# Expert weights in rows of 8 KB, gate products ahead of up products, and two sets of transposes moved

## The chip, the cores and the metric

The kernel runs on one core of a Trainium2 chip. The metric is the device time of one execution in microseconds (us). Three runs of the kernel before gave 740.38, 738.9 and 739.66 us.

## The reference

One decoder block and a final norm, for 256 tokens of width 1024, in float32. The first half is adaptive RMSNorm, one input projection (5120 columns), two kinds of attention with 8 heads each, gated branches and an output projection. The second half, cut to what matters here:

```python
h2 = modulate(rms_norm(x, g2), shift2, scale2)
scores = sigmoid(h2 @ w_router)              # 64 experts in 8 groups, the best 4 groups, the best 8 experts
for each expert e, for the tokens that chose it:
    y[e] = (silu(h2 @ w_gate[e]) * (h2 @ w_up[e])) @ w_down[e]   # 1024 -> 256 -> 1024
moe = sum over e of weight[token, e] * y[e] + the same with one shared expert
out = rms_norm(x + gate2 * moe, final_g)
```

The weights of one expert are three matrices of 1 MB each, so the 64 experts read 192 MB.

## The kernel before

**Tiles.** The chosen (token, expert) pairs are put into slots. 26 tiles hold 128 slots each: most take two experts with 64 slots each, every fourth or fifth takes four experts with 32 slots (tile 3, 7, 11, 15, 20 and 25), some take one of 96 and one of 32. Which expert has how many slots is decided on the chip by rank. `groups(i)` lists the column ranges of a tile: two groups of 64, or four of 32.

**A tile's work**, in the loop at the end of the file: `tile_up` (L1131, TensorE) multiplies the tile's gathered tokens `hl` with the gate and up weights into one PSUM buffer `gu` of 512 columns, 256 for each; `swiglu` (ACT L1003, DVE L1004) makes the gated values `sg`; `slot_map` (L1141 and DVE) makes the tile's scatter matrix; `scatter` (L1187) adds the results of the tile before to the sums; `gather(i + 1)` (L1071, 96 short bf16 matmuls) collects the tokens of the next tile, copied out by `hl<-rot` on ACT and DVE (L1075, L1077); `hidden_T` (L1016) transposes `sg`, and DVE copies it to `at` (L1019); `down` (L1155) multiplies `at` with the down weights. In tile 0 the gather of tile 1 stands behind `down`. `extra` adds the ranking in tile 0, the shared expert's transposes in tile 1, its end in tile 11, and the ranking of late experts in tile 15. The shared expert's up products (`shared_up`, L1011) run earlier, with the attention's last work.

**Weights.** `w8()` hands out buffers of 1 MB (8 KB on each of 128 partitions) in a ring, first 9 and in the expert part 20 of them; some are buffers of earlier work (`vv`, `hh`, `g2r`, `gr`, `sr`, `xs`, `whi`, `wlo`), which come free when that work is done. All weight DMAs are issued by SyncE (SP) in the order of the program. At most 8 of them are in flight, since each waits for the one eight ahead of it. SP waits before a DMA until the ring's buffer is free, and everything behind it waits too.

**The start.** `mod_sums(j)` (L360) adds the conditioning vector's products, each with 1 MB of weights; `shift_scale` copies the sums on ACT (L366) and turns them with short matmuls (L370); `turned(j)` (L351) transposes two blocks of the first tokens; `modulated(j)` applies shift and scale (ACT L381, DVE); `row_hi` and `row_lo` split the projection weights into two parts (L392 and DVE), and `proj_row` (L272, L273, L275) multiplies. Their order is a written list, `do(...)`.

Of the kernel before, what the change touches and what calls it, by code (L numbers as in the profile page):

```python
# [9 lines left out]
F32 = mybir.dt.float32  # L10
# [4 lines left out]
AF = mybir.ActivationFunctionType  # L15
# [10 lines left out]
FF = 256  # L26
# [82 lines left out]
def block_kernel(ctx: ExitStack, tc: tile.TileContext, x, c, norm1_g, norm2_g, w_ada, b_ada, w_in,  # L109
                 w_branch_sb, w_branch_mb, w_out, w_router, router_bias, w_gate_e, w_up_e, w_down_e,  # L110
                 w_gate_sh, w_up_sh, w_down_sh, rel_bias, final_g, const_a, const_m, const_b, out):
    nc = tc.nc
    P = 128
    mm = nc.tensor.matmul
# [4 lines left out]
    wk = ctx.enter_context(tc.tile_pool(name="wk", bufs=1))  # L119
# [7 lines left out]
    def w8():  # L127
        ring.append(ring.pop(0))
        return k8(ring[-1], [P, 2048])
# [27 lines left out]

    ss2 = consts.tile([P, 10], F32, name="ss2")

    def load_gu(wg, wu, h):  # L160
        w = w8().rearrange("p (g j f) -> p g j f", g=2, j=4)
        nc.sync.dma_start(w[:, 0], wg.rearrange("(p j) f -> p j f", j=8)[:, 4 * h:4 * h + 4])
        nc.sync.dma_start(w[:, 1], wu.rearrange("(p j) f -> p j f", j=8)[:, 4 * h:4 * h + 4])
        return [w[:, :, j, :] for j in range(4)]

    def load_dn(wd):
        w = w8().rearrange("p (j n) -> p j n", j=2)
# [3 lines left out]
    h2, h2v, hp3, r1, h2T, scores_ = [], [], [], [], [], []  # L171
# [31 lines left out]
    with ExitStack() as pa:  # L203
        ps = pa.enter_context(tc.tile_pool(name="ps", bufs=2, reuse_waits="tile", space=PSUM))

        def big():
            return ps.tile([P, 512], F32, name="big", tag="big", bufs=4)
# [92 lines left out]
        graw, rows = {}, {}  # L300
# [53 lines left out]
        def mod_sums(j):  # L354
# [4 lines left out]
            for n in range(4):  # L359
                mm(rows["m"][32 * n:32 * n + 32, :], cpad[:, j, :], w[:, 512 * n:512 * n + 512], start=j == 0,  # L360
                   stop=j == 7, skip_group_check=True)

        def shift_scale():

            sb = wk.tile([P, 512], F32, name="adasb", tag="ada", bufs=2)
            nc.scalar.activation(sb, rows.pop("m"), AF.Copy)  # L366
            p = big()
            firsts = ident.rearrange("p (n r) -> p n r", r=32)[:, :, 0]
            for k in range(4):
                mm(p[:, 4 * k:4 * k + 4], sb[:, 128 * k:128 * k + 128], firsts, start=True, stop=True,  # L370
                   skip_group_check=True)
            p = p[:, 0:16].rearrange("p (k i u) -> p i u k", k=4, i=2)
            m = modq.rearrange("p (u k) i -> p u k i", u=2)
            bq = biasq.rearrange("p (u k) i -> p u k i", u=2)
            nc.vector.tensor_tensor(m[:, :, :, 1], p[:, 0], bq[:, :, :, 1], op=OP.add)
            nc.vector.tensor_tensor(m[:, :, :, 0], p[:, 1], bq[:, :, :, 0], op=OP.add)
            nc.vector.tensor_tensor(modq[:, :, 2], modq[:, :, 0], gb[:, 0:8], op=OP.mult)
# [312 lines left out]
        def do(f, *args, keys=()):  # L690
            plan.append((keys, lambda: f(*args)))
# [5 lines left out]
        do(mod_sums, 2, keys=[("adk", 2)])  # L697
        do(columns, keys=[("ca",)])
        for j in range(3, 8):
            if j > 3:  # L700
                do(turned, 2 * j - 8)
            do(mod_sums, j, keys=[("adk", j)])
        do(shift_scale)
        do(modulated, 0)
        do(row_hi, 0, keys=[("inj", 0)])
        do(row_lo, 0)
# [32 lines left out]
        for i, ticks in enumerate(ROW_AT):  # L739
            n = 4 + i  # L740
# [214 lines left out]
    def late_expert(k):  # L955

        no = sm("no", [1, 2], I32)
        nc.sync.dma_start(no[:, 0:1], ranks_d[:, bass.ds(k, 1)])
        rank_ = nc.values_load(no[0:1, 0:1], engines=[EN.SP], min_val=0, max_val=NE - 1)
        nc.sync.dma_start(no[:, 1:2], order_d[:, bass.ds(rank_, 1)])  # L960
        col = sm("col", [P, 4])
        nc.sync.dma_start(col, late_d[:, bass.ds(rank_, 1)].rearrange("p o q -> p (o q)"))
        ev = nc.values_load(no[0:1, 1:2], engines=[EN.SP], min_val=0, max_val=NE - 1)
        wg, wu, wd = (w[0, bass.ds(ev, 1)].rearrange("o a b -> (o a) b") for w in (w_gate_e, w_up_e, w_down_e))
        gu = load_gu(wg, wu, 0) + load_gu(wg, wu, 1)
        wd = load_dn(wd)
        for first in (0, 128):
            one = small().rearrange("p (t s) -> p t s", t=4)[:, 0:2]
            for t in range(NT):
                nc.vector.tensor_scalar(one[:, t], iota1, float(first), col[:, t:t + 1], op0=OP.add, op1=OP.is_equal)  # L970
            S = wk.tile([P, NT, 128], BF, name="S", tag="zs", bufs=4)
            nc.vector.tensor_copy(S, one)
            xg = gather(len(TILES), S)
            pq = rot()
            for t in range(NT):
                nc.tensor.transpose(pq[:, t * 128:(t + 1) * 128], one[:, t], ident)
            for t in range(NT):
                mm(pq[:, 256:257], one[:, t], col[:, 2 + t:3 + t], start=t == 0, stop=t == 1, skip_group_check=True)
            ST = wk.tile([P, 256], F32R, name="ST", tag="e", bufs=3)
            wsl = sm("wsl", [P, 1], bufs=2)  # L980
            nc.vector.tensor_copy(ST, pq[:, 0:256])
            nc.vector.tensor_copy(wsl, pq[:, 256:257])
            p = gub()
            for j in range(8):
                mm(p, xg[:, j], gu[j], start=j == 0, stop=j == 7)
            at = hidden_T(swiglu(p))
            scatter(ST, down(at, [wd], [(0, 128, 0)], wsl))

    shp, shw = {}, {}

    def load_shared():
        shw["gu"] = load_gu(w_gate_sh[0], w_up_sh[0], 0) + load_gu(w_gate_sh[0], w_up_sh[0], 1)

    def load_shared_down():
        shw["d"] = load_dn(w_down_sh[0])
# [11 lines left out]
    def shared_up(t, j0, j1):  # L1007
        if j0 == 0:
            shp[t] = rot() if t else gub()
        for j in range(j0, j1):  # L1010
            mm(shp[t], h2T[0][:, j, t * 128:(t + 1) * 128], shw["gu"][j], start=j == 0, stop=j == 7)  # L1011

    def hidden_T(sg, at=None):
        pt = rot()
# [73 lines left out]
    def load_tile(i):  # L1088
        n = len(TILES[i])
        es = []  # L1090
        for _, r in TILES[i]:
            if r < NFIX:
                es.append([w[0, r] for w in (w_gate_e, w_up_e, w_down_e)])
            else:
                ev = nc.values_load(order[0:1, r:r + 1], engines=[EN.SP], min_val=0, max_val=NE - 1)
                es.append([w[0, bass.ds(ev, 1)].rearrange("o a b -> (o a) b") for w in (w_gate_e, w_up_e, w_down_e)])
        if i == len(TILES) - 1:

            gu = [load_gu(e[0], e[1], 0) for e in es]
            ws = [w8().rearrange("p (g j f) -> p g j f", g=2, j=4) for e in es]  # L1100
            for j in (0, 2):
                for w, e in zip(ws, es):
                    for g in range(2):
                        nc.sync.dma_start(w[:, g, j:j + 2],
                                          e[g].rearrange("(p j) f -> p j f", j=8)[:, 4 + j:6 + j])
            for g, w in zip(gu, ws):
                g += [w[:, :, j, :] for j in range(4)]
            return gu, load_dn_cuts([e[2] for e in es])
        gu = [[] for s in range(n)]
        for h in range(2):  # L1110
            for s in range(n):
                gu[s] += load_gu(es[s][0], es[s][1], h)
        return gu, [load_dn(e[2]) for e in es]

    def groups(i):

        out, c0 = [], 0
        for s, (cap, _) in enumerate(TILES[i]):
            for n in (32, 32, 32) if cap == 96 else (cap,):
                out.append((c0, n, s))  # L1120
                c0 += n
        return out

    def tile_up(i, xg, gu, between=()):
        p = gub()
        for j in range(8):
            if j == 4:
                for f in between:
                    f()
            for c0, n, s in groups(i):  # L1130
                mm(p[c0:c0 + n, :], xg[:, j, c0:c0 + n], gu[s][j], start=j == 0, stop=j == 7, skip_group_check=True)  # L1131
        return swiglu(p)

    def slot_map(i):
# [87 lines left out]
    S = slots(0)  # L1222
# [11 lines left out]
    xg = gather(0, S)  # L1234
# [40 lines left out]
    for i in range(len(TILES)):  # L1275
        if i == SH_AT:
            load_shared_down()
        gu, wd = load_tile(i)
        last = i == len(TILES) - 1
        if last:  # L1280
            fin, res = final_row()
            ST, wsl = slot_map(i)
            sg = tile_up(i, xg, gu, [lambda: scatter(*prev), lambda: final_gain(fin)])
            nc.scalar.preload_act_table_set("sqrt_and_others")
        else:
            sg = tile_up(i, xg, gu, () if i else [by_expert])
            S = slots(i + 1)
            ST, wsl = slot_map(i)
            if prev:
                scatter(*prev)  # L1290
            if i:
                xg = gather(i + 1, S)
        at = hidden_T(sg)
        for f in extra.get(i, ()):
            f()
        if last:
            last_down(at, wd, groups(i), wsl, ST)
        else:
            prev = ST, down(at, wd, groups(i), wsl)
            if i == 0:  # L1300
                xg = gather(i + 1, S)
    final_norm(fin, res)
    pc.close()

# [30 lines left out]
```

## Time and profile before

| | |
|---|---|
| median of 3 runs | 739.66 us |
| lowest, highest | 738.9, 740.38 us |
| the profiled execution | 740.37 us |
| its span in the trace | 738.6 us |
| TensorE busy | 691.3 us (94%) |
| TensorE's mean granted clock | 0.989 |
| bytes by DMA | 266.73 MB, mean 361 GB/s |

The span is the time from the first to the last instruction that the profiler saw; the execution is 1.8 us longer. A resource that is busy 94% of a span need not be the one that ends last in each stretch of it, so the rows below go by stretches.

### The profile page before, as it was taken

The page shows a single profiled execution, that of the slowest core. Times are in us where ns is not written, and L with a number is a line of the kernel's source. Part 1 is how long each engine was busy: PE and PEld are TensorE (multiplying, and loading weights), DVE is VectorE, ACT ScalarE, POOL GpSimd, SP SyncE. Part 2 cuts the span into 40 slices and gives each one's busy share as a digit, 9 for nine tenths or more (in the row PEclk, how much of TensorE's full clock was granted, in tenths as well). Part 3 has the DMA queues.
Part 4 walks back from the last instruction along what each step waited for, and adds up shares of the span by engine and source line. Part 5 has one row for each costly group of instructions (what it writes and reads, how often), then busy time and mean ns, then how long its engine had stood idle before and what let it go on. Part 6 is the DMA issues. An engine that isn't in the chain of part 4 may idle for free.

```text
span 738.6 us, 12518 instructions
## 1 busy us (share of the span) xinstructions
PE 691.3 (94%) x4743; PEld 384.3 (52%) x4743; DVE 316.2 (43%) x667; ACT 202.2 (27%) x332; POOL 16.0 (2%) x33
## 2 busy tenths in 40 slices
PE   3899999999999999999999999999989998899994
PEld 0486677676888546444444454344444553355532
DVE  1366766666576833333333333233233332233323
ACT  2344666555835521111111111111111111111122
POOL 1010001000001000000000000000000000000000
PEclk9899999999999999999999999999999999999998
DMA  9999988777567699999999999999999999999994
GB/s 354 412 385 387 364 271 301 251 269 273 177 235 269 259 375 416 354 389 412 409 415 414 413 390 412 411 412 412 416 413 412 412 412 415 412 411 408 402 335 158
DMA packets 76862, 266.73 MB, mean 361 GB/s; under 512 B 7013, under 2 KB 9221, under 8 KB 67968
## 3 DMA queue, kind: packets, MB, share of 16 engines
q1 hardware_dynamic: 75344, 262.24, 91.7%
q0 software_dynamic: 1312, 3.65, 1.5%
q8 instruction: 39, 0.64, 0.4%
q14 instruction: 23, 0.19, 0.1%
q10 hardware_dynamic: 144, 0.00, 0.0%
HBM read 264.68 MB, written 1.19 MB: 360 GB/s over the span
## 4 chain that ended last, share of the span: by engine, by line
PE 51%; DMA 45%; DVE 2%; ACT 1%; issue 0%; SPq 0%; DVEq 0%; ACTq 0%
DMA w<-in_w_up_e_dram 17%; PE gu L1131 9%; PE big L272 7%; PE big L275 7%; PE big L273 7%; DMA wlo<-in_w_up_e_dram 7%; DMA sr<-in_w_down_e_dram 5%; PE rot L1155 4%; DMA w<-in_w_down_e_dram 4%; DMA hh<-in_w_down_e_dram 4%; DMA w<-in_w_ada_dram 4%; PE rot L1071 3%; DMA gr<-in_w_up_e_dram 3%; PE acc L1187 3%; PE att L420 2%; DMA hh<-in_w_gate_e_dram 2%
## 5 line engine op out<-in xcount | busy, mean ns | idle before, releaser
L1131 PE MATMUL gu<-w,hl 128*32 128x512 f32 (+1 forms) x568 | 99.0, 594 | 2.4 <-DMA w<-in_w_up_e_dram 2.0
L272 PE MATMUL big<-whi,hh 128*128 128x512 f32 x184 | 75.2, 409 | 1.7 <-ACT whi L392 1.7
L273 PE MATMUL big<-whi,hl 128*128 128x512 f32 x184 | 72.9, 396 | 0.0
L1004 DVE TENSOR_TENSOR sg<-sg,gu 128x256 f32<-128x256 f32 x27 | 11.4, 421 | 138.7 <-ACT sg L1003 138.7
L1071 PE MATMUL rot<-S,qksb 128*128 128x128 bf16 x624 | 69.1, 219 | 0.0
L1071 PE MATMUL rot<-S,qkmb 128*128 128x128 bf16 x624 | 68.7, 219 | 0.0
L1167 ACT ACTIVATE mg<-y 128x512 fp32r<-128x512 f32 x51 | 32.1, 629 | 130.2 <-DVE y L1161 130.2
L1161 DVE SCALAR_TENSOR_TENSOR y<-rot,wsl,gate 128x512 f32<-128x512 f32 (+1 forms) x53 | 39.1, 738 | 65.0 <-PE rot L1155 63.1
L1131 PEld LDWEIGHTS gu<-w,hl 128*32 128x32 f32 (+1 forms) x568 | 29.9, 121 | 60.9 <-issue 58.8
L1155 PE MATMUL rot<-w,at 128*32 128x512 f32 (+1 forms) x256 | 56.2, 610 | 5.7 <-DVE at L1019 5.7
L254 DVE TENSOR_TENSOR wlo<-w,whi 128x2048 fp32r<-128x2048 f32 x23 | 52.7, 2291 | 20.1 <-ACT whi L253 19.1
L275 PE MATMUL big<-wlo,hh 128*128 128x512 f32 x184 | 54.2, 395 | 0.2 <-DVE wlo L254 0.2
L1187 PE MATMUL acc<-mg,ST 128*128 128x512 f32 x204 | 54.0, 406 | 0.0
L1168 DVE TENSOR_TENSOR mg<-y,mg 128x512 fp32r<-128x512 f32 x51 | 35.3, 692 | 38.4 <-ACT mg L1167 38.4
L1075 ACT ACTIVATE hl<-rot 128x512 f32<-128x512 f32 x26 | 15.5, 597 | 120.8 <-PE rot L1071 120.8
L1003 ACT ACTIVATE sg<-gu 128x256 f32<-128x256 f32 x27 | 10.4, 383 | 138.5 <-PE gu L1131 138.5
L1071 PEld LDWEIGHTS <-qksb 128*128 128x128 bf16 x624 | 42.6, 98 | 7.8 <-issue 6.7
L1187 PEld LDWEIGHTS acc<-mg,ST 128*128 128x128 f32 x204 | 36.3, 188 | 17.4 <-ACT sg L1003 9.1
L253 ACT ACTIVATE whi<-w 128x2048 fp32r<-128x2048 f32 x23 | 43.9, 1909 | 5.0 <-PE big L273 5.0
L272 PEld LDWEIGHTS big<-whi,hh 128*128 128x128 f32 x184 | 35.1, 191 | 17.1 <-issue 3.8
L1071 PEld LDWEIGHTS <-qkmb 128*128 128x128 bf16 x624 | 43.6, 98 | 0.0
L275 PEld LDWEIGHTS big<-wlo,hh 128*128 128x128 f32 x184 | 34.8, 190 | 8.4 <-DVE wlo L254 0.6
(352 smaller groups left out, 1055.7 us busy)
## 6 DMA issues: line engine op xcount, KB each, us to landing
w<-in_w_gate_e_dram SPq DMA_DIRECT2D x60, 512.0 KB, 12.1
w<-in_w_up_e_dram SPq DMA_DIRECT2D x60, 512.0 KB, 12.6
w<-in_w_down_e_dram SPq DMA_DIRECT2D x26, 1024.0 KB, 12.5
w<-in_w_ada_dram SPq DMA_DIRECT2D x24, 1024.0 KB, 11.6
w<-in_w_in_dram SPq DMA_DIRECT2D x16, 1024.0 KB, 12.4
whi<-in_w_gate_e_dram SPq DMA_DIRECT2D x12, 512.0 KB, 11.3
whi<-in_w_up_e_dram SPq DMA_DIRECT2D x12, 512.0 KB, 11.7
wlo<-in_w_down_e_dram SPq DMA_DIRECT2D x6, 1024.0 KB, 11.3
```

The source lines that it names most:

```text
L253: nc.scalar.activation(hi, w, AF.Copy)
L254: nc.vector.tensor_tensor(lo, w, hi.bitcast(F32), op=OP.subtract)
L272: mm(p, aa[i][0], ww[i][0], start=start and i == 0, stop=False)
L273: mm(p, aa[i][1], ww[i][0], start=False, stop=False)
L275: mm(p, aa[i][0], ww[i][1], start=False, stop=stop and i == n - 1)
L1071: mm(p[:, b * 128:(b + 1) * 128], hp3[k // 3][k % 3][:, half * 4 + b, :], S[:, k // 3], start=k == 0, stop=k == 5)
L1131: mm(p[c0:c0 + n, :], xg[:, j, c0:c0 + n], gu[s][j], start=j == 0, stop=j == 7, skip_group_check=True)
L1155: mm(py[c0:c0 + w, 0:n], at[:, jj, c0:c0 + w], wd[s][:, jj, o:o + n], start=jj == 0, stop=jj == 1, skip_group_check=True)
L1161: nc.vector.scalar_tensor_tensor(y, py[:, 0:n], wsl, gate2[:, o:o + n], op0=OP.mult, op1=OP.mult)
L1167: nc.scalar.activation(yh, y, AF.Copy)
L1168: nc.vector.tensor_tensor(yl, y, yh.bitcast(F32), op=OP.subtract)
L1187: mm(sums(t, c), m if len(y) > 1 else m.bitcast(F32), part, start=False, stop=stop and k == len(y) - 1, skip_group_check=True)
```

## The change

1. `load_gu` gives the gate and the up matrix of an expert a 1 MB buffer each, and moves each with one DMA whose rows are 8 KB long. Before, a buffer held half of both: two DMAs of 512 KB with rows of 4 KB. `load_tile` issues all gates of a tile, then all ups, then the downs. For the last tile the ups come in pieces of 4, 2 and 2 of the 8 blocks.
2. `up_cut` makes the products with 256 columns each, all eight gate blocks first, then the eight up blocks; before, each product had 512 columns (gate and up side by side).
3. In the start, the first `turned` goes ahead of `mod_sums(4)`, the other three behind the last `mod_sums`, around `shift_scale`, whose copy on ACT is a step of its own (`mod_copy`).
4. `hidden_T` stands ahead of `gather(i + 1)`, in all tiles, and tile 0's gather for tile 1 ahead of its ranking and its `down`.

```diff
-    def load_gu(wg, wu, h):
-        w = w8().rearrange("p (g j f) -> p g j f", g=2, j=4)
-        nc.sync.dma_start(w[:, 0], wg.rearrange("(p j) f -> p j f", j=8)[:, 4 * h:4 * h + 4])
-        nc.sync.dma_start(w[:, 1], wu.rearrange("(p j) f -> p j f", j=8)[:, 4 * h:4 * h + 4])
-        return [w[:, :, j, :] for j in range(4)]
+    def load_gu(wg, wu):
+
+        ws = [w8().rearrange("p (j f) -> p j f", j=8) for _ in range(2)]
+        for w, d in zip(ws, (wg, wu)):
+            nc.sync.dma_start(w, d.rearrange("(p j) f -> p j f", j=8))
+        return ws
+
+    def up_cut(p, xg, gu, gs, k):
+
+        g, j = divmod(k, 8)
+        for c0, n, s in gs:
+            mm(p[c0:c0 + n, FF * g:FF * g + FF], xg[:, j, c0:c0 + n], gu[s][g][:, j, :], start=j == 0, stop=j == 7,
+               skip_group_check=True)
...
         for j in range(3, 8):
-            if j > 3:
-                do(turned, 2 * j - 8)
+            if j == 4:
+                do(turned, 0)
             do(mod_sums, j, keys=[("adk", j)])
+
+        do(mod_copy)
+        do(turned, 2)
         do(shift_scale)
+        do(turned, 4)
+        do(turned, 6)
         do(modulated, 0)
...
-            gu = [load_gu(e[0], e[1], 0) for e in es]
-            ws = [w8().rearrange("p (g j f) -> p g j f", g=2, j=4) for e in es]
-            for j in (0, 2):
-                for w, e in zip(ws, es):
-                    for g in range(2):
-                        nc.sync.dma_start(w[:, g, j:j + 2],
-                                          e[g].rearrange("(p j) f -> p j f", j=8)[:, 4 + j:6 + j])
-            for g, w in zip(gu, ws):
-                g += [w[:, :, j, :] for j in range(4)]
+            gu = [[w8().rearrange("p (j f) -> p j f", j=8) for g in range(2)] for e in es]
+            for g, o, m in ((0, 0, 8), (1, 0, 4), (1, 4, 2), (1, 6, 2)):
+                for w, e in zip(gu, es):
+                    nc.sync.dma_start(w[g][:, o:o + m], e[g].rearrange("(p j) f -> p j f", j=8)[:, o:o + m])
             return gu, load_dn_cuts([e[2] for e in es])
-        gu = [[] for s in range(n)]
-        for h in range(2):
-            for s in range(n):
-                gu[s] += load_gu(es[s][0], es[s][1], h)
+        gu = [[w8().rearrange("p (j f) -> p j f", j=8) for g in range(2)] for e in es]
+        for g in range(2):
+            for w, e in zip(gu, es):
+                nc.sync.dma_start(w[g], e[g].rearrange("(p j) f -> p j f", j=8))
...
-            if i:
-                xg = gather(i + 1, S)
         at = hidden_T(sg)
+        if not last:
+            xg = gather(i + 1, S)
         for f in extra.get(i, ()):
             f()
         if last:
             last_down(at, wd, groups(i), wsl, ST)
         else:
             prev = ST, down(at, wd, groups(i), wsl)
-            if i == 0:
-                xg = gather(i + 1, S)
```

`shared_up`, the late expert's products and `tile_up` call `up_cut` in a loop over k from 0 to 15.

SP's DMAs for tile 2 and the first of tile 3, before (tile 2's two experts lie in `hh`, `g2r` and two buffers of `gr`; tile 3 begins at `vv`):

```order
L162 DMA hh<-in_w_gate_e_dram 128x1024
L163 DMA hh<-in_w_up_e_dram 128x1024
L162 DMA g2r<-in_w_gate_e_dram 128x1024
L163 DMA g2r<-in_w_up_e_dram 128x1024
L162 DMA gr_2449<-in_w_gate_e_dram 128x1024
L163 DMA gr_2449<-in_w_up_e_dram 128x1024
L162 DMA gr_2452<-in_w_gate_e_dram 128x1024
L163 DMA gr_2452<-in_w_up_e_dram 128x1024
L168 DMA sr<-in_w_down_e_dram 128x2048
L168 DMA xs<-in_w_down_e_dram 128x2048
```

The same place now:

```order
L1122 DMA hh<-in_w_gate_e_dram 128x2048
L1122 DMA gr_2483<-in_w_gate_e_dram 128x2048
L1122 DMA g2r<-in_w_up_e_dram 128x2048
L1122 DMA gr_2484<-in_w_up_e_dram 128x2048
L176 DMA sr<-in_w_down_e_dram 128x2048
L176 DMA xs<-in_w_down_e_dram 128x2048
L1122 DMA vv<-in_w_gate_e_dram 128x2048
L1122 DMA w_2671<-in_w_gate_e_dram 128x2048
L1122 DMA w_2673<-in_w_gate_e_dram 128x2048
L1122 DMA w_2675<-in_w_gate_e_dram 128x2048
L1122 DMA w_2670<-in_w_up_e_dram 128x2048
L1122 DMA w_2672<-in_w_up_e_dram 128x2048
```

The DMA into `g2r` now stands behind the first one into `gr`, and a tile's buffers are no longer filled in the order of the ring: `w_2675`, the seventh buffer from `vv` on, is filled fourth.

TensorE at the start, before (`big` takes the sums of `mod_sums`, `att<-ca` are the transposes of `turned`, `big<-ca` those of `shift_scale`):

```order
L360 MATMUL big<-w_112,cpad 32x512 x4
L351 MATMUL att<-ca,gr_102 128x128 x4
L360 MATMUL big<-w_114,cpad 32x512 x4
L351 MATMUL att<-ca,gr_102 128x128 x4
L360 MATMUL big<-w_116,cpad 32x512 x4
L351 MATMUL att<-ca,gr_102 128x128 x4
L360 MATMUL big<-w_118,cpad 32x512 x4
L351 MATMUL att<-ca,gr_102 128x128 x4
L360 MATMUL big<-w_125,cpad 32x512 x4
L370 MATMUL big<-ca,adasb 128x4 x4
```

The same place now:

```order
L368 MATMUL big<-w_112,cpad 32x512 x4
L359 MATMUL att<-ca,gr_102 128x128 x4
L368 MATMUL big<-w_114,cpad 32x512 x4
L368 MATMUL big<-w_116,cpad 32x512 x4
L368 MATMUL big<-w_118,cpad 32x512 x4
L368 MATMUL big<-w_125,cpad 32x512 x4
L359 MATMUL att<-ca,gr_102 128x128 x4
L380 MATMUL big<-ca,adasb 128x4 x4
L359 MATMUL att<-ca,gr_102 128x128 x8
L280 MATMUL big<-whi,hh 128x512
```

Twelve of the sixteen transposes now stand behind the last of the sums, four of them ahead of the short matmuls and eight behind.

TensorE in an early tile, before: the end of the gather (`qkmb` and `qksb` are halves of the tokens' values), the transposes of `sg`, and the first of the down products (`gr` holds down weights here):

```order
L1071 LDWEIGHTS qkmb_1943
L1071 MATMUL rot<-S,qkmb_1943 128x128
L1016 MATMUL rot<-ca,sg 128x128 x2
L1155 MATMUL rot<-gr_2833,at 32x512 x3
L1155 MATMUL rot<-gr_2835,at 32x512
```

The same tile now, from the end of the scatter on:

```order
L1196 MATMUL acc_1948<-mg,ST 128x512
L1196 MATMUL acc_1950<-mg,ST 128x512
L1031 MATMUL rot<-ca,sg 128x128 x2
L1086 LDWEIGHTS qksb_1804
L1086 MATMUL rot<-S,qksb_1804 128x128
```

The two transposes moved from behind the gather to ahead of it.

## Rows read from the trace of the kernel before

**Rows 1.** The page: DMA's busy tenths in 40 slices of the span.
```profile
DMA  9999988777567699999999999999999999999994
```

**Rows 2.** Windows: us, busy of PE, PEld, DVE, ACT, POOL; PE clock; DMA share; GB/s.
```profile
264.00:324.00 60.00, 57.60 (x414) 27.59 (x409) 19.69 (x48) 7.86 (x15) 0.00 (x0) 0.97 1.00 384
324.00:684.00 360.00, 342.16 (x2760) 164.78 (x2759) 116.84 (x263) 44.80 (x80) 1.09 (x2) 1.00 1.02 411
...
700.00:712.00 12.00, 11.48 (x91) 5.11 (x89) 4.53 (x9) 1.86 (x3) 0.20 (x1) 1.00 0.92 318
```

**Rows 3.** The chain that ended last, one tile: start us, us, what.
```profile
655.40 6.87 PE gu L1131 x32
...
664.97 2.70 PE rot L1071 x48
668.47 3.65 PE rot L1155 x16
672.13 6.87 PE gu L1131 x32
```

**Rows 4.** Waits of TensorE: us in total, times, longest us.
```profile
PE rot L1155 <- DVE at L1019: 10.9, 21, 0.5
...
PE gu L1131 <- DMA w<-in_w_up_e_dram: 2.0, 2, 1.5
```

**Rows 5.** Timeline of TensorE: first up products of tiles 0, 1, 11, 12, 25.
```profile
261.21 1.08 PE L1131 MATMUL gu<-w,hl 128*64 128x512 f32 x4
...
280.42 2.01 PE L1131 MATMUL gu<-w,hl 128*64 128x512 f32 x8 [0.39 <-DVE hl L1077]
...
448.83 1.49 PE L1131 MATMUL gu<-w,hl 128*32 128x512 f32 x12
...
474.63 0.64 PE L1131 MATMUL gu<-wlo,hl 128*64 128x512 f32 x1
...
706.15 1.06 PE L1131 MATMUL gu<-w,hl 128*32 128x512 f32 x8
```

**Rows 6.** Windows: no weights in flight; 4 KB rows alone; a slow patch; 8 KB alone.
```profile
252.00:256.50 4.50, 4.50 (x18) 2.14 (x17) 3.98 (x9) 0.74 (x1) 0.00 (x0) 1.00 0.02 4
...
381.00:389.00 8.00, 8.00 (x84) 2.32 (x76) 2.04 (x3) 1.39 (x3) 0.00 (x0) 1.00 1.03 410
441.00:445.00 4.00, 3.73 (x54) 3.23 (x52) 1.12 (x4) 0.53 (x1) 0.00 (x0) 1.00 1.00 296
453.00:457.00 4.00, 4.00 (x42) 1.30 (x34) 0.16 (x1) 0.39 (x1) 0.00 (x0) 1.00 1.01 422
```

**Rows 7.** Timeline of SP: DMA issues into three buffers.
```profile
243.94 0.33 SPq L162 DMA_DIRECT2D g2r<-in_w_gate_e_dram  x1
...
255.87 0.33 SPq L162 DMA_DIRECT2D gr<-in_w_gate_e_dram  x1
...
279.50 0.33 SPq L162 DMA_DIRECT2D w<-in_w_gate_e_dram  x1
```

**Rows 8.** Timeline of TensorE: passes of 256 columns in the last tile's down.
```profile
723.78 0.40 PE L1155 MATMUL rot<-hh,at 128*32 128x256 f32 x1
...
724.02 0.38 PE L1155 MATMUL rot<-hh,at 128*32 128x256 f32 x1
...
724.24 0.59 PE L1155 MATMUL rot<-hh,at 128*32 128x256 f32 x2
```

**Rows 9.** Timeline of TensorE: attention's last matmuls, first and seventh of a run.
```profile
236.93 0.39 PE L273 MATMUL big<-late,hl 128*128 128x512 f32 x1
...
238.31 0.39 PE L273 MATMUL big<-late,hl 128*128 128x512 f32 x1
```

**Rows 10.** Timeline of TensorE, and a window: the start.
```profile
29.01 1.45 PE L370 MATMUL big<-ca,adasb 128*128 128x4 f32 x8 [0.72 <-ACT adasb L366]
...
32.11 0.79 PE L272 MATMUL big<-whi,hh 128*128 128x512 f32 x1 [1.65 <-ACT whi L392]
...
31.00:34.30 3.30, 2.19 (x5) 1.45 (x6) 2.65 (x6) 3.30 (x7) 0.00 (x0) 0.50 1.03 411
```

More of the change, by code (lines that the diff above doesn't have):

```diff
@@ L361, in mod_sums, with mod_copy @@
                    stop=j == 7, skip_group_check=True)
+        def mod_copy():
+            sb = rows["c"] = wk.tile([P, 512], F32, name="adasb", tag="ada", bufs=2)
+            nc.scalar.activation(sb, rows.pop("m"), AF.Copy)
         def shift_scale():
-            sb = wk.tile([P, 512], F32, name="adasb", tag="ada", bufs=2)
-            nc.scalar.activation(sb, rows.pop("m"), AF.Copy)
-            p = big()
+            sb, p = rows.pop("c"), big()
             firsts = ident.rearrange("p (n r) -> p n r", r=32)[:, :, 0]
@@ L964, in late_expert @@
         wg, wu, wd = (w[0, bass.ds(ev, 1)].rearrange("o a b -> (o a) b") for w in (w_gate_e, w_up_e, w_down_e))
-        gu = load_gu(wg, wu, 0) + load_gu(wg, wu, 1)
+        gu = load_gu(wg, wu)
         wd = load_dn(wd)
@@ L983, in late_expert @@
             p = gub()
-            for j in range(8):
-                mm(p, xg[:, j], gu[j], start=j == 0, stop=j == 7)
+            for k in range(16):
+                up_cut(p, xg, [gu], [(0, 128, 0)], k)
             at = hidden_T(swiglu(p))
@@ L991, in load_shared @@
     def load_shared():
-        shw["gu"] = load_gu(w_gate_sh[0], w_up_sh[0], 0) + load_gu(w_gate_sh[0], w_up_sh[0], 1)
+        shw["gu"] = load_gu(w_gate_sh[0], w_up_sh[0])
     def load_shared_down():
@@ L1009, in shared_up @@
             shp[t] = rot() if t else gub()
-        for j in range(j0, j1):
-            mm(shp[t], h2T[0][:, j, t * 128:(t + 1) * 128], shw["gu"][j], start=j == 0, stop=j == 7)
+        for k in range(2 * j0, 2 * j1):
+            up_cut(shp[t], h2T[0][:, :, t * 128:(t + 1) * 128], [shw["gu"]], [(0, 128, 0)], k)
     def hidden_T(sg, at=None):
@@ L1125, in tile_up @@
         p = gub()
-        for j in range(8):
-            if j == 4:
+        for k in range(16):
+            if k == 8:
                 for f in between:
                     f()
-            for c0, n, s in groups(i):
-                mm(p[c0:c0 + n, :], xg[:, j, c0:c0 + n], gu[s][j], start=j == 0, stop=j == 7, skip_group_check=True)
+            up_cut(p, xg, gu, groups(i), k)
         return swiglu(p)
```

## Prediction

> **What bounds the kernel now.** I read the page first: TensorE is busy for 94% of the span (the table), and the DMA row shows nines until slice 7, a thinner middle, and nines again from slice 14 to 38 [rows 1]. So two resources are nearly full, and which of them ends last has to be read by stretch. Then the stretches of the expert part: DMA share 1.00 from 264 to 324, 1.02 from 324 to 684 at 411 GB/s, and 0.92 at 318 GB/s when the last tile's pieces are issued [rows 2]. A share of 1.00 says that the sixteen engines always have packets; only a faster packet or a smaller total can shorten that stretch.
>
> TensorE is as near. A tile with no wait takes 672.13 - 655.40 = 16.73 us [rows 3]: products up 6.87, the scatter of the tile before 2.0, the next tile's gather 2.70, a gap, the down products 3.65. The gap is the step on which the third part of the change works: the gather ends at 664.97 + 2.70 = 667.67 and the down products start at 668.47; between them lie two transposes and the wait for DVE's copy of them, 21 times and 10.9 us in all [rows 4]. From tile 0 (261.21) to tile 25 (706.15) pass 444.94 us [rows 5]; 25 tiles of 16.73 would be 418.25. Of the 26.7 over, tile 0 has 280.42 - 261.21 - 16.73 = 2.5, and tile 11 with the shared expert's end 474.63 - 448.83 - 16.73 = 9.1. Of the 15.1 left I put 3 on other inserted work (an estimate: the shared transposes and the late-expert ranking) and **12 on waiting for weights**. The waits view's largest row of such waits has only 2.0 us [rows 4], because a matmul that starts late between its neighbours counts as busy; I trust the starts.
>
> So TensorE waits for weights late, while the DMA queue never rests: **the end is set by the weight stream**, with TensorE about 12 us behind it as the second bound.
>
> **The change, part by part.** The base is the profiled execution, 740.37 us (0.7 over the median of the runs, 739.66; I subtract it at the end).
>
> *Weights in 8 KB rows.* The trace has stretches with one kind alone: 410 GB/s where all in flight are gate and up halves with 4 KB rows, 422 where all are down weights with 8 KB rows [rows 6]. For 1 MB (1,048,576 bytes) that is 2.557 us against 2.485, 0.073 us less. The stream's steady part moves two of these for each expert of tiles 3 to 24 (54 experts), two for tile 2, four for the last tile: about 114 MB. 114 x 0.073 = **-8.3 us**. The bounds are 0 (row length is not the cause, only which weights they are) and -8.3.
>
> *Slow patches.* In 441 to 445 the 4 KB rows ran at 296 GB/s [rows 6], 4 x (1 - 296/410) = 1.1 us lost; the pure down stretch shows none. From 324 to 684 a third of the bytes at 422 and two thirds at 410 would be 414; at 411 some 360 x 3/414 = 2.6 us are lost. In 264 to 324, 384 against 414 is 4.3 more, part of which is plain shortage of free buffers. I take half of the 2.6: **-1.3**, with bounds 0 and -6.9.
>
> *Order of issue.* Now all gates go out before the first up. In tile 2 the second expert's gate goes into `gr`, and the first expert's up into `g2r` behind it on SP. Before, `g2r` was filled from 243.94 and `gr` from 255.87, when the product that reads `gr` was done [rows 7]; between them the DMA engines have nothing (0.02 in 252 to 256.5, [rows 6]). The 1 MB of `g2r` used to pass before this hole; now it waits behind `gr`, and comes after it: one MB at 2.5 us, **+2.5** (0 if a buffer further on would have stopped the stream for as long anyway). In tile 3 the fourth gate takes the buffer of tile 0's first down weights; the DMA for that buffer left at 279.50 before [rows 7], and will be the fourth of the tile instead of the sixth pair, with seven others of its tile behind it. Tile 0's down will be earlier by the 2 us of its own gap, so I count **0**, between -2 and +2.
>
> *Last tile.* Its gates go as 1 MB, the ups in 4 x 512 KB and 8 x 256 KB, where 16 pieces of 256 KB were. The stretch 700 to 712 lost 12 x (1 - 318/410) = 2.7 us [rows 2]; half the small pieces are gone, but the end is still cut fine: **-1**, between 0 and -2.7.
>
> *Halved matmuls.* Each up product now runs as 16 steps of 256 columns instead of 8 of 512, per expert group. A 512-column pass (an f32 product is two records) takes 6.87/16 = 0.43 us. The trace has 256-column passes with the same 32-column f32 weights in the last tile's down: 723.78, 724.02, 724.24 [rows 8], so 0.24 for the first and 0.22 for the next, against 0.215 for half of 0.43. I take 3 ns on 32 passes, 0.1 us per tile; the upper bound is 0.24 in all, 0.85 per tile. A rule speaks against this part: the Trainium skill, "TensorEngine Tiling (Array Packing)", section "Instruction Overhead", gives each matmul some 60 cycles of overhead, which is 25 ns at 2.4 GHz, and by it the 32 added passes of a tile would cost 0.8 us, 21 us in all; the second pass of the row above shows at most 5 ns. In `shared_up`, with 128-column weights, the weight load is longer: the nearest rows, one load of 128 columns for each matmul, start (238.31 - 236.93)/6 = 0.23 apart [rows 9], where a 256-column pass that hides its load takes 0.215. 64 passes x 0.015 = **+1.0** (0 to 1.0), and it is on the path, since `gr` is freed by these products.
>
> *Transposes ahead of the gather.* TensorE's wait for `at` (10.9 us) goes under the gather, and tile 0 loses up to its 2.5. On TensorE alone -13.4; but this engine waits for weights anyway, so its gain becomes a longer wait for weights: **0** in the sum. It frees each buffer a little earlier, which the full queue can't use. If the queue had room, this would be the gain.
>
> *First tokens' transposes.* TensorE stands idle for 0.72 and 1.65 us while ACT copies the sums and makes the first weights' parts [rows 10]; four transposes go into the first gap and eight into the second. Before, twelve of the sixteen ran between sums that wait for the weights' DMA, where they cost nothing, so only an earlier rise of the granted clock (0.50 in 31 to 34.3, where the first projection matmuls start [rows 10]) can gain: **-0.5**, between -2 and +1 (if `modulated` has to wait for the last of them).
>
> Sum: -8.3 - 1.3 + 2.5 + 0 - 1 + 1.0 + 0 - 0.5 = **-7.6**: 740.37 - 7.6 = 732.8, and less the 0.7, **732**.
>
> Does TensorE stay under it? It could end 10.9 + 2.5 + 12 - 1.0 - 26 x 0.1 = 22 us earlier if no weight wait were left. I leave it 3 us of them (the four-expert tiles want 12 MB at once). 19 against 7.6: yes.
>
> **Rivals.** *A, TensorE becomes the bound (the other side).* If a 256-column pass with two 64-column groups, which no row of before shows in f32 with 128 rows, costs x more per tile, TensorE's work ends the kernel at 740.37 - (10.9 + 2.5 + 12 - 1.0) + 3 + 26x. That passes 732.8 at x = 0.53 and the time before at x = 0.82, near the first pass of [rows 8] at all 32 (0.85). At x = 1.0 it gives 745.0, less 0.7, 744. For it: the 0.24; against it: the 0.22 after it. Chance 0.08. (By the Trainium skill's 0.8 us a tile, above, this sum would give 739.)
>
> *B, the rate does not rise.* The 422 may belong to something else in those stretches than the length of a row, and the order of issue still holds the queue up: 740.37 + 2.5 - 1 + 1.0 - 0.5 - 0.7 = 741.7. With the hold-up hidden too, 739. For it: short stretches say little on cause; against it: gate, up and down weights lie in the same memory and go to the same buffers, and differ in the row. Chance 0.12.
>
> *C, slow patches belong to 4 KB rows and all go.* -6.9 in place of -1.3: 732 - 5.6 = 726.4. For it: no 8 KB stretch has one; against: the pure 8 KB stretches are short. Chance 0.15.
>
> **How the numbers follow.** The forecast has 0.65, A 0.08, B 0.12, C 0.15. A measurement of this kernel tells about 0.2% (1.5 us) from no change. The forecast's own range, from its bounds, is 728 to 737; with C at one end and half of B at the other it is 726.5 to 739.5. Faster: all of the forecast and C and a little of A: 0.82. Same: half of B and a third of A, 0.09. Slower: 0.09.
>
> **What would show it.** The windows of 324 to 684 near 420 GB/s with the share still at 1.0; the wait of the down products for DVE's copy gone, and more waits of up products for up weights instead; the tile period still 16.8 where nothing is waited for (17.6 would be A); SP's `g2r` issue after `gr`, about 256. A rate of 411 would make me wrong by B, and rows of up products waiting for nothing but running to the end by A.

## The result, and the profile after

| | before | after |
|---|---|---|
| median, us | 739.28 (4 runs, 738.42 to 740.38) | 728.72 (4 runs, 726.94 to 729.78) |
| the profiled execution, us | 740.37 | 728.46 |
| its span, us | 738.6 | 726.7 |

The ratio is 0.9854, with a 95% interval of 0.983 to 0.9878: 10.6 us faster, 1.5%. The forecast was 732 and 7.6 us faster, the range 726.5 to 739.5.

The page of the changed kernel, DMA's busy tenths in 40 slices, as in [rows 1]:

```profile
DMA  9999989777555599999999999999999999999993
```

Windows of the changed kernel (columns as in [rows 2]): the hole before the stream, the stream in its two stretches, and the last tile:

```profile
248.00:252.00 4.00, 4.00 (x25) 3.41 (x25) 3.16 (x23) 1.76 (x2) 0.00 (x0) 1.00 0.02 4
252.00:256.50 4.50, 4.50 (x25) 3.90 (x24) 4.50 (x4) 1.33 (x3) 0.00 (x0) 1.00 0.25 80
...
264.00:324.00 60.00, 59.47 (x623) 37.55 (x623) 21.75 (x52) 8.45 (x16) 0.00 (x0) 1.00 1.01 421
324.00:684.00 360.00, 349.90 (x3678) 214.95 (x3671) 119.08 (x268) 46.45 (x83) 1.58 (x3) 0.99 1.01 420
...
688.00:700.00 12.00, 12.00 (x111) 5.50 (x112) 3.62 (x7) 2.46 (x5) 0.00 (x0) 1.00 0.89 321
```

The same share of busy engines now moves 420 GB/s where it moved 411, and 421 where it moved 384 [rows 2]. The cut pieces of the last tile still run at 321. The hole begins earlier than before: in 248 to 252 next to nothing moves, where the kernel before still had 252 GB/s:

```profile
248.00:252.00 4.00, 4.00 (x18) 2.38 (x18) 2.99 (x20) 2.45 (x3) 0.00 (x0) 1.00 0.62 252
```

The chain of the changed kernel, one tile with no wait, and TensorE's waits (columns as in [rows 3] and [rows 4]):

```profile
325.03 6.91 PE gu L171 x128
...
334.87 2.68 PE rot L1086 x48
337.55 3.57 PE rot L1164 x32
341.12 6.91 PE gu L171 x128
```

```profile
PE gu L171 <- DMA hh<-in_w_up_e_dram: 1.9, 1, 1.9
PE gu L171 <- DMA w<-in_w_up_e_dram: 1.9, 1, 1.9
PE gu L171 <- DMA wlo<-in_w_up_e_dram: 1.9, 1, 1.9
PE gu L171 <- DMA sr<-in_w_up_e_dram: 1.6, 1, 1.6
```

The down products start where the gather ends (334.87 + 2.68 = 337.55), the wait for DVE's copy is gone, and a tile takes 16.09 us instead of 16.73. At least a part of what TensorE won there it waits for up weights instead: the four rows above add to 7.3 us, and all the rows of such waits in the kernel before to 5.3. (By this view a matmul that starts late between its neighbours counts as busy, so both are lower bounds.)

SP's issues at tile 2 in the changed kernel (timeline), against [rows 7]:

```profile
237.71 0.33 SPq L1122 DMA_DIRECT2D hh<-in_w_gate_e_dram  x1
254.02 0.33 SPq L1122 DMA_DIRECT2D gr<-in_w_gate_e_dram  x1
254.45 0.37 SPq L1122 DMA_DIRECT2D g2r<-in_w_up_e_dram  x1
```

`g2r` now leaves behind `gr`, as the order of the rows in the section on the change says: 16.3 us without an issue of a weight DMA, where the kernel before had 11.6 (from 244.32 to 255.87).

### The profile page after: what moved, and what is told of

The parts are those of the page before. It is cut to its first block, busy times and chain, and to the rows that moved or that the text cites. A ratio compares the mean times of both kernels' runs of the same rounds, so it can differ in the third digit from the quotient of the medians.

```text
span 726.7 us, 14358 instructions
## 1 busy us (share of the span) xinstructions
PE 688.4 (95%) x5927; PEld 448.0 (62%) x5927; DVE 316.8 (44%) x667; ACT 202.3 (28%) x332; POOL 15.8 (2%) x33
## 3 DMA queue, kind: packets, MB, share of 16 engines
q0 software_dynamic: 1312, 3.65, 1.5%
## 4 chain that ended last, share of the span: by engine, by line
PE 64%; DMA 33%; DVE 1%; ACT 1%; issue 0%; SPq 0%; DVEq 0%; ACTq 0%
PE gu L171 14%; DMA w<-in_w_up_e_dram 8%; PE big L280 7%; PE big L283 7%; PE big L281 7%; PE rot L1164 6%; PE rot L1086 6%; DMA sr<-in_w_up_e_dram 5%; PE acc L1196 4%; DMA w<-in_w_ada_dram 4%; DMA whi<-in_w_gate_e_dram 3%; DMA w<-in_w_down_e_dram 3%; DMA whi<-in_w_down_e_dram 3%; DMA vv<-in_w_down_sh_dram 3%; DMA hh<-in_w_up_e_dram 3%; PE att L430 2%
## 5 line engine op out<-in xcount | busy, mean ns | idle before, releaser
L171 PE MATMUL gu<-w,hl 128*32 128x256 f32 (+1 forms) x1136 | 118.7, 383 | 2.1 <-DMA w<-in_w_up_e_dram 1.9
L171 PEld LDWEIGHTS gu<-w,hl 128*32 128x32 f32 (+1 forms) x1136 | 68.8, 122 | 42.2 <-issue 5.1
L171 PE MATMUL gu<-whi,hl 128*64 128x256 f32 (+1 forms) x208 | 49.6, 397 | 0.5 <-DMA whi<-in_w_up_e_dram 0.5
L171 PE MATMUL gu<-wlo,hl 128*32 128x256 f32 (+1 forms) x256 | 46.1, 393 | 1.9 <-DMA wlo<-in_w_up_e_dram 1.9
L1086 PEld LDWEIGHTS <-qksb 128*128 128x128 bf16 x624 | 44.9, 98 | 0.4
L280 PEld LDWEIGHTS big<-whi,hh 128*128 128x128 f32 x184 | 34.6, 188 | 16.2 <-issue 3.8
```

Of the source, the lines that this page charges most:

```text
L171: mm(p[c0:c0 + n, FF * g:FF * g + FF], xg[:, j, c0:c0 + n], gu[s][g][:, j, :], start=j == 0, stop=j == 7, skip_group_check=True)
L280: mm(p, aa[i][0], ww[i][0], start=start and i == 0, stop=False)
L1086: mm(p[:, b * 128:(b + 1) * 128], hp3[k // 3][k % 3][:, half * 4 + b, :], S[:, k // 3], start=k == 0, stop=k == 5)
```

## The experiments

**Does the length of a row set the rate, or the bytes of a DMA?** Three kernels change only the DMAs of gate and up weights in tiles 0 to 24 of the changed kernel.

```diff
-                nc.sync.dma_start(w[g], e[g].rearrange("(p j) f -> p j f", j=8))
+                for q in (0, 4):
+                    nc.sync.dma_start(w[g][:, q:q + 4], e[g].rearrange("(p j) f -> p j f", j=8)[:, q:q + 4])
```

> The changed kernel, but each gate and up matrix of tiles 0 to 24 comes as two DMAs of 512 KB with 4 KB rows (blocks 0 to 3, then 4 to 7). Row-length theory: the stream falls back to about 411 GB/s with slow patches near 295, so most of the gain goes: 737 to 739 us. Rival (the order of issue, the moves and the new buffers give the gain): 728 to 730 us.

```diff
+                nc.sync.dma_start(w[g].rearrange("p (h j) f -> p h j f", h=2),
+                                  e[g].rearrange("(h p j) f -> p h j f", h=2, j=4))
```

> The changed kernel, but each gate and up matrix of tiles 0 to 24 comes in one DMA of 1 MB whose rows are 4 KB (two from each partition's two places in memory). The rows of these matrices reach other partitions, so the products are other numbers; the work is the same. Row-length theory: 411 GB/s, 736 to 739 us, as with two DMAs of 4 KB rows. Rival (bytes per DMA): 728 to 730 us.

```diff
+                for q in (0, 64):
+                    nc.sync.dma_start(w[g][q:q + 64], e[g].rearrange("(p j) f -> p j f", j=8)[q:q + 64])
```

> The changed kernel, but each gate and up matrix of tiles 0 to 24 comes as two DMAs of 512 KB that keep the 8 KB rows (partitions 0 to 63, then 64 to 127). Row-length theory: 420 GB/s stays, 728 to 730 us. Rival (bytes per DMA, with at most 8 in flight, set the rate): like the 4 KB halves, 737 to 739 us.

Measured: two DMAs with 4 KB rows 737.3 us (ratio 0.9984, 0.9969 to 0.9999); one DMA of 1 MB with 4 KB rows 736.96 (0.9971, 0.9954 to 0.9988); halves of the partitions with 8 KB rows 1064.26 (1.4379, 1.4251 to 1.4507). The windows of the three, in this order:

```profile
324.00:684.00 360.00, 345.84 (x3626) 211.21 (x3620) 117.98 (x263) 45.43 (x81) 1.58 (x3) 0.98 1.02 411
```

```profile
324.00:684.00 360.00, 343.99 (x3620) 210.79 (x3614) 117.01 (x262) 45.45 (x81) 1.09 (x2) 0.99 1.02 412
```

```profile
324.00:684.00 360.00, 248.41 (x2206) 141.80 (x2206) 66.88 (x150) 25.17 (x46) 0.00 (x0) 0.82 1.01 244
```

With 4 KB rows the rate is 411 and 412 whether a DMA has 512 KB or 1 MB, and the gain is nearly all lost; between these two sizes the bytes of a DMA don't count. Going to 8 KB rows is worth 0.0130 or 0.0117 of 739 us: 9.6 or 8.7 us. (A third of the bytes in each of these windows are down weights, which have 8 KB rows on 128 partitions in all of the kernels.) The third kernel can't speak to the question: with its gate and up weights going to 64 partitions at a time the stream runs at 244, little more than half the rate, so it brought a loss of its own, and neither theory foresaw it.

**The transposes of the gated values.** Alone on the kernel before; taken out of the changed kernel; and, in the changed kernel, kept in tile 0 alone:

```diff
-            if i:
-                xg = gather(i + 1, S)
         at = hidden_T(sg)
+        if not last:
+            xg = gather(i + 1, S)
...
-            if i == 0:
-                xg = gather(i + 1, S)
```

> The kernel before, with only the transposes of the gated values moved ahead of the gather (and tile 0's gather ahead of its down). Theory (the weight stream sets the end): the wait for DVE's copy, 10.9 us, goes, the waits for up weights grow by about as much, and the time is 738 to 740 us. Rival (TensorE sets the end): 727 to 730 us.

> The changed kernel with the transposes of the gated values back behind the gather. Theory (TensorE has some 20 us of waits for weights to spare): 728 to 730 us, with the waits for up weights smaller by about 10 us. Rival (after the faster rows TensorE is the bound): 735 to 739 us.

```diff
+            if i:
+                xg = gather(i + 1, S)
         at = hidden_T(sg)
-        if not last:
+        if i == 0:
             xg = gather(i + 1, S)
```

> The changed kernel with the transposes behind the gather again in tiles 1 to 24; only tile 0 has its transposes and the gather of tile 1 ahead of its down. Theory (what the move gives is the earlier freeing of tile 0's buffers, so that the stream doesn't run dry near 300 us): all of it stays, 728 to 730 us. Rival (the 0.5 us in every tile counts): 730.5 to 731.5 us, as with the move undone.

Measured: alone 735.99 (0.9968, 0.9954 to 0.9982), 2.4 us faster, against the theory's 0 to 1 and far from the rival's 10. Taken out of the changed kernel, 731.08 (0.9888, 0.9862 to 0.9914): by the medians 2.4 us of the gain lost, by the ratios 2.5, with intervals that overlap a little. Kept in tile 0 alone, 728.23 (0.9859, 0.9838 to 0.9881), as the changed kernel beside it on the same chip (727.9, below). So the 0.5 us in each of the other tiles counts for nothing that these times show (0.3 us, with some 2 us of uncertainty), and the move in tile 0 for all. Windows of 296 to 324, in the order before, alone, taken out, tile 0 alone, changed:

```profile
296.00:324.00 28.00, 27.48 (x207) 11.91 (x204) 9.86 (x23) 3.88 (x7) 0.00 (x0) 1.00 0.98 357
```

```profile
296.00:324.00 28.00, 28.00 (x256) 14.43 (x256) 8.72 (x23) 3.22 (x6) 0.00 (x0) 1.00 1.02 410
```

```profile
296.00:324.00 28.00, 27.48 (x313) 16.98 (x310) 9.39 (x23) 3.77 (x7) 0.00 (x0) 1.00 0.97 374
```

```profile
296.00:324.00 28.00, 27.48 (x319) 17.29 (x316) 9.39 (x23) 3.31 (x7) 0.00 (x0) 1.00 1.02 418
```

```profile
296.00:324.00 28.00, 28.00 (x338) 17.59 (x338) 9.09 (x23) 3.22 (x6) 0.00 (x0) 1.00 1.01 420
```

Without the move the stream runs short there (357 and 374), with it in tile 0 it doesn't (410, 418, 420). In 28 us, 357 against 410 is 3.6 us lost, 374 against 420 is 3.1. The mean busy share, 0.97 and 0.98, hardly shows it; windows of 2 us do (the kernel before, then the one with the move taken out):

```profile
302.00:304.00 2.00, 2.00 (x12) 0.59 (x10) 0.00 (x0) 0.00 (x0) 0.00 (x0) 1.00 0.84 252
```

```profile
314.00:316.00 2.00, 2.00 (x44) 1.17 (x36) 1.24 (x3) 0.63 (x1) 0.00 (x0) 1.00 0.82 250
```

The stream is waiting there for buffers that the first tiles free: with the move taken out, SP issues no weights from 287.6 to 296.74, when tile 1's down products have read `wlo`. The next timelines show the same further on, SP's first DMA for tile 5 (into `sr`), with the move taken out and in the changed kernel:

```profile
313.50 0.33 SPq L1122 DMA_DIRECT2D sr<-in_w_gate_e_dram  x1
```

```profile
308.83 0.33 SPq L1122 DMA_DIRECT2D sr<-in_w_gate_e_dram  x1
```

What the move brings forward is not tile 0's own down, though, but tile 1. TensorE's rows of tile 0 and the first of tile 1, in the kernel before (with a window for the granted clock) and in the changed one:

```profile
271.31 0.27 PE L946 MATMUL rot<-cpad,permb 64*64 64x256 bf16 x1 [0.66 <-DVE scr L1147]
...
271.97 5.27 PE L1155 MATMUL rot<-w,at 128*64 128x512 f32 x16
```

```profile
272.00:276.00 4.00, 4.00 (x13) 1.25 (x14) 0.84 (x2) 0.38 (x1) 0.00 (x0) 0.59 1.01 360
```

```profile
259.38 3.67 PE L171 MATMUL gu<-w,hl 128*64 128x256 f32 x32
...
272.12 3.65 PE L1164 MATMUL rot<-w,at 128*64 128x512 f32 x16
275.60 0.38 PE L171 MATMUL gu<-w,hl 128*64 128x256 f32 x1
```

Counted from tile 0's first up product (261.21 before [rows 5], 259.38 now), its down starts 10.8 us later before and 12.7 us later now, since the gather stands ahead of it. But tile 1's first up product comes 16.2 us after tile 0's, where it came 19.2 (280.42 before, [rows 5]): 3.0 us earlier. The kernel with tile 0's move alone has 16.2 too, and the one with the move taken out 19.2. Of the 3.0, 1.6 are the granted clock: the same sixteen products of the down take 5.27 us where the clock is 0.59 of full in the mean (the lower level, 1.2 GHz, for a part), and 3.65 at full. Before them TensorE had stood idle for 0.66 us, waiting for DVE in the ranking; with the gather in that place it doesn't wait. The slow down, 5.27 to 5.35 us, is in three of the four profiled executions with the old order and in none of the ten with the gather ahead; the fourth (in the kernel with the first tokens' transposes alone) has the same wait and the full clock, so the wait alone doesn't settle it.

**The order of the ring.** A tile's buffers are taken in the order in which its DMAs go out; or the DMAs go out in the order of the ring:

```diff
-        gu = [[w8().rearrange("p (j f) -> p j f", j=8) for g in range(2)] for e in es]
+        gu = list(zip(*[[w8().rearrange("p (j f) -> p j f", j=8) for e in es] for g in range(2)]))
```

> The changed kernel, but a tile's buffers are taken from the ring in the order in which its DMAs are issued (all gates, then all ups), so that tile 2's first two gates go to hh and g2r and only its ups wait for gr; tile 3's fourth gate takes the fourth buffer. Theory (the 1 MB behind gr costs 2.5 us of an idle queue): 2 to 3 us below the changed kernel, 726 us. Rival (another buffer would have stopped the stream as long): as the changed kernel, 728 to 729 us.

> The version with buffers taken in the order of issue, beside the changed kernel on one chip. Theory (one MB no longer waits for gr): 1 to 3 us below the changed kernel of the same runs. Rival: within 0.5 us of it.

> The changed kernel as it is, beside the others on one chip: 728 to 730 us, a ratio near 0.985.

```diff
-        for g in range(2):
-            for w, e in zip(gu, es):
+        for w, e in zip(gu, es):
+            for g in range(2):
```

> The changed kernel, but the 1 MB DMAs of a tile go out as gate and up of the first expert, gate and up of the second, and so on, which is also the order of the ring. Theory (slow patches near 295 GB/s at a full share come with gate and up rows fetched in turn, not with 4 KB rows): patches come back, 2 to 4 us over the version with buffers in the order of issue. Rival (they belong to 4 KB rows and that order together): no patches, within 1 us of that version.

Measured: the order of the ring 727.18 (0.9836, 0.9813 to 0.9859) at first. Then, on one chip: the changed kernel 727.9 (0.9858, 0.9834 to 0.9881), the order of the ring again 725.97 (0.9839, 0.9815 to 0.9863), gate and up in pairs 726.07 (0.9836, 0.9811 to 0.9861). By the medians and the ratios all three are some 1.3 to 1.9 us under the changed kernel, though the intervals overlap. The edit changes the order of buffers in all tiles, so tile 3's part in it isn't told apart from tile 2's. SP's timeline in the version with the order of the ring:

```profile
238.70 0.33 SPq L1122 DMA_DIRECT2D hh<-in_w_gate_e_dram  x1
243.00 0.33 SPq L1122 DMA_DIRECT2D g2r<-in_w_gate_e_dram  x1
255.01 2.84 SPq L1122 DMA_DIRECT2D gr<-in_w_up_e_dram  x2
```

`g2r` is filled ahead of the hole again. From the first issue into `gr` to the end of the span this version has 724.0 - 255.0 = 469.0 us, the changed kernel 726.7 - 254.0 = 472.7: 3.7 us less (3.1 against the changed kernel's other profiled execution, 472.1), of which 1.0 us is given back because `gr` came free that much later in this execution. The 1 MB that now passes ahead of the hole accounts for 2.5 of them, by the rate of 420 GB/s.

The pairs were tried for the slow patches of [rows 6]. Windows of 384 to 444 in the kernel before, in the one with the transposes alone, and in the one with two DMAs of 4 KB rows:

```profile
384.00:444.00 60.00, 58.45 (x515) 28.71 (x507) 19.69 (x46) 7.11 (x13) 0.00 (x0) 1.00 1.02 405
```

```profile
384.00:444.00 60.00, 59.76 (x503) 28.51 (x500) 20.47 (x42) 8.58 (x15) 0.00 (x0) 1.00 1.02 406
```

```profile
384.00:444.00 60.00, 59.30 (x667) 36.50 (x665) 20.60 (x42) 8.58 (x15) 0.00 (x0) 1.00 1.02 412
```

The patch stays when only the transposes move and is gone with the new buffers and order, though the rows are 4 KB again (one shorter dip, 372 GB/s in 676 to 680, is left there). The pairs with 8 KB rows show none either (420 in 324 to 684). So neither the row's length alone nor the turn of gate and up alone makes it; what does stays open. The two together, and a half of each matrix in one buffer, are left, and weren't tried.

**The first tokens' transposes**, alone on the kernel before:

```diff
-            if j > 3:
-                do(turned, 2 * j - 8)
+            if j == 4:
+                do(turned, 0)
             do(mod_sums, j, keys=[("adk", j)])
+        do(mod_copy)
+        do(turned, 2)
         do(shift_scale)
+        do(turned, 4)
+        do(turned, 6)
...
```

> The kernel before, with only the first tokens' transposes moved. Theory (the granted clock stays at full in 27 to 38 us, and all that follows, the freeing of gr and with it the stream too, comes 1.9 us earlier): 737 to 738 us, a ratio near 0.9975. Rival (the stream hides it): 739 to 739.5 us.

Measured: 738.06 (0.9981, 0.9965 to 0.9997), 1.4 us faster, with an interval from 0.2 to 2.6. Windows of the start, first the changed kernel, then this one:

```profile
27.40:31.00 3.60, 3.43 (x28) 2.17 (x20) 0.41 (x3) 1.05 (x2) 0.00 (x0) 1.00 1.03 409
31.00:34.30 3.30, 2.50 (x9) 1.63 (x10) 3.09 (x7) 3.30 (x8) 0.00 (x0) 1.00 1.03 411
```

```profile
27.40:31.00 3.60, 3.60 (x19) 2.06 (x11) 0.00 (x0) 0.60 (x1) 0.00 (x0) 0.50 1.02 409
31.00:34.30 3.30, 3.30 (x13) 2.50 (x13) 2.03 (x7) 2.25 (x5) 0.00 (x0) 0.50 1.03 408
```

In the changed kernel's profiled execution the granted clock stays at full through the start; with the same order of instructions, this one has half of it (1.2 GHz) for the whole stretch. The first issue into `gr`, which shows what the start was worth, came at 254.02 in the one and 255.61 in the other, and 255.87 before. So the theory of the expectation, that the order settles the clock and brings 1.9 us, falls: the clock in the start varies between executions of one order. Over the profiled executions, `gr` was issued at 255.87, 255.02 and 256.09 with the old order (mean 255.7), and between 254.02 and 256.96 with the new (11 of them, mean 255.1). That is 0.6 us between means with much scatter; the size of this part is 0.2 to 2.6 us by the times, and no closer. This execution is also the one in which tile 0's down ran at the full clock, which the edit doesn't touch (tile 1 follows tile 0 by 17.6 us in it, against 19.2), so the 1.4 us need not all come from the start.

**Rows and order alone**: the changed kernel with both moves of transposes undone.

> The changed kernel without its two moves: only the 8 KB rows with the gates first and the 256-column products. Theory (the stream sets the end and gets 13 us from its rate, less 2.5 for the order): 730 to 732 us, the wait for DVE's copy still there. Rival (the moves of the transposes carry the gain): 736 to 739 us.

Measured: 732.21 (0.9906, 0.988 to 0.9932), 6.9 us faster. Its wait for DVE's copy, from the waits view (in this kernel's line numbers), is as before:

```profile
PE rot L1160 <- DVE at L1030: 10.9, 21, 0.5
```

The three parts alone give 6.9 + 2.4 + 1.4 = 10.7 us, and all together 10.6: they add up, within intervals of 1.0 to 1.9 us on each of the three.

## Why the prediction came out as it did

**The stream sets the end: right.** Every part that acts on the stream showed in the time, and the 0.5 us per tile of TensorE's time did not (tile 0 alone keeps all the gain). The reading of the busy share was too strong: a mean of 1.00 over 264 to 324 was taken to say that packets never ran out, and in 302 to 304 of the same stretch it is 0.84.

**8 KB rows, -8.3: right.** 420 GB/s where 411 was; the two kernels with 4 KB rows put it at 8.7 and 9.6 us. All that the changed rows and order bring by themselves, 6.9 us, is close to the forecast's sum for these terms, -8.3 - 1.3 + 2.5 - 1 + 1.0 = -7.1. That closeness is in part luck: the smaller terms aren't each confirmed, and the 1.0 for `shared_up` is mis-sized. Its first and last groups of products, in the kernel before and in the one with the rows and order alone, are as far apart:

```profile
241.18 3.65 PE L1011 MATMUL gu<-vv,gr 128*128 128x512 f32 x8
...
254.70 3.60 PE L1011 MATMUL rot<-w,gr 128*128 128x512 f32 x8
```

```profile
241.32 3.67 PE L171 MATMUL gu<-vv,gr 128*128 128x256 f32 x16
...
254.91 3.62 PE L171 MATMUL rot<-w,gr 128*128 128x256 f32 x16
```

From the first start to the last end that is 17.12 and 17.21 us, so the halved products cost 0.1 us here.

**Order of issue, +2.5: right in its mechanism.** The hole is there, `g2r` stands behind `gr`, and taking the buffers in order wins 1.3 to 1.9 us by the times, 3.1 to 3.7 by the stream of single executions.

**The transposes ahead of the gather, 0: this step failed.** I had reasoned that a buffer freed earlier is of no use to a full queue. The queue was full over 324 to 684, but not in 296 to 324, where it ran at 357 with the buffers of the first tiles still in use. I had seen the loss (384 in 264 to 324) and had even called part of it a shortage of free buffers, but booked it under slow patches of 4 KB rows and took none of it. It was worth 2.4 us, and tile 0's part of the move is all of it. This is most of the 3 us between the forecast's gain and the measured one. The 2.5 us that I gave tile 0 on TensorE were nearly right (3.0), but I had put them on its gap alone and on an earlier down of tile 0; about half of what was won there was the granted clock, and what came earlier is tile 1. The sign that I named, a tile period of 16.8, had left the 0.5 us of this part out; it is 16.09.

**Slow patches, -1.3, and rival C:** they went, but C's cause is wrong for the two stretches it was built on. Nearly all of the loss in 264 to 324 was the shortage of buffers (with the transposes moved alone and 4 KB rows kept, 296 to 324 runs at 410); the patch near 441 vanishes with 4 KB rows too. Its cause is open.

**First tokens' transposes, -0.5:** the size is inside what was measured (0.2 to 2.6), but the mechanism, an earlier rise of the clock, comes in some executions only. A size that fits without its mechanism is luck.

**Halved matmuls, 0.1 per tile: right, a little high.** The up products take 6.91 us against 6.87. Passes of 256 columns in the changed kernel (timeline, three of a tile's four column groups):

```profile
324.85 0.39 PE L171 MATMUL gu<-wlo,hl 128*32 128x256 f32 x3
...
325.06 0.39 PE L171 MATMUL gu<-wlo,hl 128*32 128x256 f32 x3
...
325.28 0.39 PE L171 MATMUL gu<-wlo,hl 128*32 128x256 f32 x3
```

They start 0.215 apart, so rival A had no ground. The Trainium skill ("TensorEngine Tiling (Array Packing)", "Instruction Overhead") puts some 60 cycles of overhead on each matmul, from which the prediction's estimate was 0.8 us on a tile; measured are 0.04, and the measurement decides. (The estimate counts 32 added passes; the column groups of a tile run side by side, as the x3 at one start above shows, so only 16 are added one behind the other, and by that count the estimate is 0.4 us, still ten times what was measured.)

**Rival B** fell with 420 GB/s. **The last tile, -1,** wasn't tried by itself: the cut pieces run as slowly as before (321 GB/s over 688 to 700, where 700 to 712 had 318), so what this part gave stays open.

Two slips of reading on which nothing rests: the row of busy tenths [rows 1] has nines in its first five slices only and eights in the next two, and 0.24 us on 32 passes is 0.81 us over the 6.87, where the prediction has 0.85.

## What to carry to other kernels

Where a stream of weights sets the end, look at its rate in windows of a few us, not in the mean over a long stretch: the places where it falls below its best with buffers short, here in the first tiles of the loop, are where work on the engines still counts, and here one early tile was worth as much as the move in all of them. Try longer contiguous rows for DMAs (8 KB moved 420 GB/s here where 4 KB moved 411; longer ones weren't tried), and take ring buffers in the order in which their DMAs are issued, since one DMA that waits for its buffer holds up all behind it. The two versions that do all of this are the fastest here, at 725.97 us (0.9839) and 726.07 (0.9836) beside 727.9 for the changed kernel.

## What the runs showed of the hardware

A stream whose gate and up weights go in DMAs of 512 KB to 64 partitions with 8 KB rows moves 244 GB/s with all engines busy (share 1.01); one with DMAs of the same size to 128 partitions with 4 KB rows moves 411 (both with a third of their bytes in down weights, 1 MB to 128 partitions). I had taken the two to be equal but for the row. In the first, TensorE, waiting for weights, had a mean granted clock of 0.82 over 324 to 684. And the granted clock differs between executions of the same order of instructions: 1.00 and 0.50 in the start, full and half in tile 0's down.
